# Small products of the heads, placed one by one between the products of a weight stream

## The chip, the cores and the metric

The kernel runs on one core of one Trainium2 chip. The metric is device time in microseconds. The kernel before takes 2738.81 us (median of 3 runs, 2738.59 to 2742.34).

TensorE (PE) multiplies and writes to PSUM; VectorE (DVE), ScalarE (ACT) and GpSimd (POOL) work on SBUF and PSUM; SyncE (SP) issues the transfers. Each engine takes its instructions in order and waits on semaphores of the others.

## The reference

Two layers of a decoder are computed for a prompt of 256 tokens and eight samples of 8 tokens, 320 columns in all, with shared weights. All is float32.

```python
def mixer(h, s_gla, buf, pos0, w_in, ...):
    proj = h @ w_in                       # q, k, v, g, gates, pooling input
    ...
    o, s_new = gla(q, k, v, gk, s_gla)    # 4 heads, state 128 x 256 a head
    o = rmsnorm(o, gla_norm).reshape(B, T, GLA_WIDTH) * jax.nn.silu(g)
    p, buf_new = pool_mixer(u, buf, pos0, w_pool, pool_scale)
    out = jnp.concatenate([o, p.astype(o.dtype)], axis=-1) @ w_out
    return out, s_new, buf_new

def gla step:                             # by chunk of tokens
    o_intra = einsum('bhij,bhjv->bhiv', scores, vi)
    o_inter = einsum('bhid,bhdv->bhiv', qi * exp(b), S)
    S_new = exp(b_last)[..., None] * S + einsum('bhjd,bhjv->bhdv', k_dec, vi)

def layer:
    x = x + mixer(rmsnorm(x, norm_mix[l]), ...)
    h = rmsnorm(x, norm_ffn[l])
    x = x + (silu(h @ w_gate[l]) * (h @ w_up[l])) @ w_down[l]
```

The width of the model is 2048, a head's v is 256 wide and its k 128, the FFN is 5632 wide. Outputs are the tokens, the heads' states of the prompt and of each sample, and the pooling buffers.

## The kernel before

Activations are held transposed: a tile is 128 features by 320 tokens. A *unit* is a block of weights, four row tiles by 256 columns (512 KB), which serves two output tiles. To keep float32 accuracy at the rate of a shorter format, a weight block is split into a high and a low part (`hl`): ScalarE makes the high part (L109), VectorE the low part (L110). Each product is then three matmuls, high by high, high by low, low by high (`mm3`, L145 to L147), of 320 columns each: a unit of four row tiles has 2 x 4 x 3 = 24 of them. These are the *stream products* (`acc<-xh,hl` and the like in the rows).

`run` goes through the list of units. For unit i it issues the loads of weights up to five units ahead, the split of unit i + 2, the evictions that are due, the 24 matmuls, and then `step`, which lets every generator in `gens` go on to its next `yield`. So the work that isn't part of the stream is issued between units, in the order in which the generators stand in the list. The order is fixed when the program is built; there is no scheduler.

The heads' work is such a generator (`head_gen`), one for each of four heads in each layer. It issues on TensorE:

- ten transposes of v (`ps_vt`, `ps_vs`, `ps_vq`, L651 to L657);
- three units later the output `ps_o`, in two halves of 128 rows: a product of 64-row weights (L700), eight products of 8 columns, one for a sample's state each (L702), and two for the prompt (L704, 256 columns, and L705, 128 columns); behind them two state products of 512 columns (`ps_sn`, L683). A plain float32 product shows as two passes in the rows;
- two units later the sum of squares for the head's norm (`ps_or`, L716), two products of the prompt's state (`ps_sp`, L719) and two more state products.

The other engines follow in between: ScalarE copies v and o out of PSUM (L667 to L670, L710, L711) and the prompt's state (L724), VectorE updates the samples' states (`S`, L691), `rsqrt` makes the norm (L133 to L138), GpSimd multiplies (L730). With the last step `st["head"]` is counted up, and the next head may load its states and transpose.

`gate_gen` multiplies a head's o with silu(g) (GpSimd, L748) and, a unit later, splits the product into `oh` and `ol` (L120, L125). The units of `w_out` come after those of `w_in`: first four units that read the pooling half (`ph`, `pl`), then four that read the gated heads (`oh`, `ol`), and so on.

The PSUM tiles of the small work come from a pool of four (`smt`), those of the stream from another of four.

Of the kernel before, what the change touches and what calls it, by code (L numbers as in the profile page):

```python
# [35 lines left out]
# columns of `vecs`, one 128-row column per feature tile  # L36
# [5 lines left out]
# pairs of 128-column tiles of w_in, in the order in which they are multiplied  # L42
# [10 lines left out]


class Unit:
    """A block of weights: nk row tiles by 256 columns, used by two output tiles."""
# [7 lines left out]
class Decoder:  # L64
    def __init__(self, tc, ctx, a):
        self.tc, self.nc, self.a = tc, tc.nc, a
        nc = self.nc
        pool = lambda name, bufs, **k: ctx.enter_context(tc.tile_pool(name=name, bufs=bufs, **k))
        self.const = const = pool("const", 1)
        self.act = pool("act", 1)  # L70
        self.ffb = pool("ffb", 2)
        self.wp = pool("wp", 1)
        self.nrm = pool("nrm", 1)
        self.keep = pool("keep", 1)
        self.acc = pool("acc", 4, space=PSUM)
        self.sm = pool("sm", 4, space=PSUM)

        self.vecs = const.tile([P, V_N], F32, name="vecs")
        nc.sync.dma_start(out=self.vecs, in_=a["vecs"])
        self.xT = self.act.tile([P, KT, T], F32, name="xT")  # L80
        self.xh = self.act.tile([P, KT, T], F32R, name="xh")
        self.xl = self.act.tile([P, KT, T], F32R, name="xl")
        self.ident = const.tile([P, P], F32, name="ident")
        self.ones = const.tile([P, P], F32, name="ones")
        self.masks = const.tile([P, 5 * 128 + 256], U8, name="masks")
        small = const.tile([P, 8], F32, name="small")
        self.sel4, self.warm, self.eps = small[:, 0:4], small[:, 4:5], small[:, 5:6]
        self.wcnt = const.tile([P, 4, 16], F32, name="wcnt")
        self.sc = self.keep.tile([P, H, 384], F32, name="sc")
        self.scs = self.keep.tile([64, H, 64], F32, name="scs")  # L90
        nc.gpsimd.memset(self.eps, EPS)
        self.last_sq, self.mf = [], None
        self.units = []
        self.gens = []
        self.later = []

# [8 lines left out]
    def split(self, hi, lo, src, scale=None):  # L105
        """hi + lo = src * scale, each of them with the 12 bits that the array multiplies."""
        nc = self.nc
        if scale is None:
            nc.scalar.copy(hi, src)  # L109
            nc.vector.tensor_tensor(lo, src, hi.bitcast(F32), ALU.subtract)  # L110
        else:
            nc.scalar.activation(hi, src, AF.Copy, scale=scale)  # L112
            nc.vector.scalar_tensor_tensor(lo, src, scale, hi.bitcast(F32), ALU.mult, ALU.subtract)  # L113

    def split2(self, his, los, srcs, scales=(None, None)):
        """Two splits, so that neither engine waits for the other's half."""
# [12 lines left out]
    def rsqrt(self, out, src, scale):  # L129
        """out = 1 / sqrt(src * scale + EPS): exp(-log / 2), then a Newton step."""  # L130
# [18 lines left out]
    def pair_units(self, srcs, order, rhs, evac, nk=4):  # L149
        """Units that make one pair of output tiles: srcs[i] holds row tiles 4 i .. 4 i + 3."""  # L150
        box = {}
        units = []
        for n, i in enumerate(order):
            def mm(hl, n=n, i=i):
                if n == 0:
                    box["ps"] = [self.acc.tile([P, 512], F32, tag="acc", name="acc") for _ in range(2)]
                for j in range(2):
                    for k in range(nk):
                        xh, xl = rhs(i * nk + k)
                        self.mm3(box["ps"][j][:, :T], hl, k, j, xh, xl,  # L160
                                 n == 0 and k == 0, n == len(order) - 1 and k == nk - 1)
            ev = (lambda: evac([t[:, :T] for t in box["ps"]])) if n == len(order) - 1 else None
# [45 lines left out]

    def step(self):
# [7 lines left out]
    def add_square(self, m, x):  # L217
        """Adds x * x into the running sum over feature tiles."""
# [9 lines left out]
    def make_r(self):  # L228
        """After the last square: r = rsqrt(mean + eps) on every partition."""
# [7 lines left out]
    def new_x(self, ms, l, base):  # L237
        """Two tiles of x are final: the operands with the next norm's weight, and the squares."""
# [13 lines left out]
    def mixer_units(self, l):  # L252
# [22 lines left out]
        # w_out: the pooling half of the rows first  # L275
# [51 lines left out]
    def gk_gen(self, l):  # L327
        """log of the gates: P = 16 * gk = log_sigmoid(z), z = h w_gk w_gk_up + b."""
# [6 lines left out]
        # [hi | lo] of a row tile side by side: one pass multiplies both  # L335
# [31 lines left out]
    def level_gen(self):  # L367
        """Scores k_j . q_i exp(b_i - b_j) for j <= i, transposed. Tokens are halved again and
        again: at level s, a pair with i in the second and j in the first half of a group of 2 s
        takes exp(sum from the half's start to i) on q and exp(sum from j to the half's end) on k,  # L370
        so that no exponent is above zero."""
# [31 lines left out]
        for li, s in enumerate((1, 2, 4, 8, 16, 32, 64, 128)):  # L403
# [30 lines left out]
            if s == 4:  # L434
                # whole sequences of the sample group
# [45 lines left out]
        # k decayed to the end of the prompt  # L481
# [30 lines left out]
    def kd_sample(self):  # L512
        """k decayed to the end of its sequence, as 32 rows a sequence: hi, lo, hi, lo."""
# [22 lines left out]
    def stack(self, x, out, his, los):  # L536
        """x [P, n, 8, 8] into out [P, n, 8, 4, 8] as rows hi (at his) and lo (at los)."""
# [10 lines left out]
    # -- pooling  # L548
# [16 lines left out]
    def pool_gen(self, l, i, EP, ES):  # L565
# [4 lines left out]
        # sums over trailing windows, doubling; only what the last one needs  # L570
# [13 lines left out]
        # the sequence's start: fewer positions than the window  # L584
        nc.gpsimd.tensor_tensor(cp[:, :, BUF : BUF + 16], cp[:, :, BUF : BUF + 16],
                                self.wcnt[:, i : i + 1, :].to_broadcast([P, 2, 16]), ALU.mult)
        # the buffers that go on: the last 15 rows
# [35 lines left out]
    # -- values and gates, one head at a time  # L623
# [7 lines left out]
    def head_gen(self, h, vT):  # L631
# [15 lines left out]
        p1, p2, p3 = self.smt("ps_vt"), self.smt("ps_vs"), self.smt("ps_vq")  # L647
        for c in range(2):
            for t in range(2):
                o = 256 * t + 128 * c  # L650
                nc.tensor.transpose(p1[:, o : o + 128], vT[:, c, 128 * t : 128 * t + 128], self.ident)  # L651
        for c in range(2):
            nc.tensor.transpose(p2[:64, 128 * c : 128 * c + 128], vT[:, c, NP:], self.ident)
        for c in range(2):
            for t in range(2):
                o = 256 * t + 128 * c
                nc.tensor.transpose(p3[:, o : o + 128],  # L657
                                    vq[:, c, 4 * t : 4 * t + 4].rearrange("p b a t -> p (b a t)"), self.ident)
        st["turned"] += 1
        yield  # L660
# [4 lines left out]
        # rows of one sequence at a time, zero elsewhere  # L665
# [11 lines left out]
        yield  # L677

        def state_mm(qd):
            pss = []  # L680
            for half in range(2):
                pz = self.smt("ps_sn")
                nc.tensor.matmul(pz, st["kqt"][:, qd, 128 * h : 128 * h + 128],  # L683
                                 vqt[:, 2 * half : 2 * half + 2, qd, :], start=True, stop=True)
# [11 lines left out]
        pos = []  # L696
        for c in range(2):
            po = self.smt("ps_o")
            vc = slice(128 * c, 128 * c + 128)
            nc.tensor.matmul(po[:, NP:T], vs[:, vc], self.scs[:, h, :], start=True, stop=False)  # L700
            for b in range(NB):
                nc.tensor.matmul(po[:, NP + 8 * b : NP + 8 * b + 8], S[b // 4][:, b % 4, vc],  # L702
                                 st["q8"][:, h, 8 * b : 8 * b + 8], start=False, stop=(b == NB - 1))
            nc.tensor.matmul(po[:, :NP], vt[:, 0, vc], self.sc[:, h, 0:256], start=True, stop=False)  # L704
            nc.tensor.matmul(po[:, 128:NP], vt[:, 1, vc], self.sc[:, h, 256:384], start=False, stop=True)  # L705
            pos.append(po)
        pss = state_mm(0)
        yield
        for c in range(2):
            nc.scalar.activation(o[:, c, :], pos[c][:, :T], AF.Copy, scale=self.vec(l, V_GN, c))  # L710
            nc.scalar.activation(sq[:, c, :], pos[c][:, :T], AF.Square)  # L711
        nc.gpsimd.tensor_tensor(sq[:, 0, :], sq[:, 0, :], sq[:, 1, :], ALU.add)
        state_out(0, pss)
        yield
        pr = self.smt("ps_or")
        nc.tensor.matmul(pr[:, :T], self.ones, sq[:, 0, :], start=True, stop=True)  # L716
        pS = self.smt("ps_sp")
        for t in range(2):
            nc.tensor.matmul(pS[:, :DV], st["kdt"][:, t, 128 * h : 128 * h + 128], vt[:, t, :],  # L719
                             start=(t == 0), stop=(t == 1))  # L720
        pss = state_mm(1)
        yield
        sp = late.tile([P, 2, T], F32, tag="osq", name="sp")[:, 0, :DV]
# [21 lines left out]
    def gate_gen(self, ts, h):  # L745
        st = self.st
        for j, t in enumerate(ts):
# [110 lines left out]
    def build(self):  # L858
# [4 lines left out]
        # x and the first weights arrive in turn  # L863
# [8 lines left out]
        # the array's clock rises once it has been busy for a while  # L872
# [75 lines left out]
    def finish(self, evacs):  # L948
        """The last tiles of x, and the last norm."""
# [25 lines left out]
def _pairs(w, cols):  # L975
    """[L, K, N] -> [L, N/256, K/512, 128, 4 * 256]: blocks in the order of use."""
# [7 lines left out]
def _cols(v):  # L984
    """[n * 128] -> [128, n]"""
# [74 lines left out]
```

## Time and profile before

| what | value |
|---|---|
| median of the timed runs | 2738.81 us |
| profiled execution: span (the page gives no other time of it) | 2735.4 us |
| TensorE busy | 2701.1 us, 99% |
| VectorE, ScalarE, GpSimd busy | 1351.9, 1067.3, 308.4 us |
| mean granted TensorE clock | 0.985 |
| HBM | 148 GB/s over the span |

A busy TensorE here only means that instructions follow each other without a gap; at the lower of its two clock levels it is as busy. The granted clock has to be read beside it, by stretch. In the list of instructions the given duration of a matmul overlaps with the next one, so that steps from start to start, or the chain of waits, tell what one takes.

### The profile page before, as it was taken

To read this page: it belongs to the slowest core of one execution; us is meant where nothing else is said; L and a number is where in the kernel's file an instruction comes from. 1 tells how busy PE (TensorE), PEld (TensorE's weight loads), DVE (VectorE), ACT (ScalarE), POOL (GpSimd) and SP (SyncE) were. 2 spreads that over 40 slices of the span, in tenths; PEclk is the share of its full clock that TensorE was granted. 3 is DMA by queue.
4 is the path that set the end of the run, shared out by engine and by line. 5 is a ranking of instruction groups with operands and counts; after the bars stand their busy time and mean duration, and the time that the engine had idled before them with its cause. 6 is when DMAs were issued, how large, how long until landed. Compare 5 with 4: busy or idle time off the path is not lost.

```text
span 2735.4 us, 44895 instructions
## 1 busy us (share of the span) xinstructions
PE 2701.1 (99%) x19046; PEld 2680.6 (98%) x19046; DVE 1351.9 (49%) x1654; ACT 1067.3 (39%) x1344; POOL 308.4 (11%) x347
## 2 busy tenths in 40 slices
PE   8999999999999999999999999999999999999997
PEld 8999999999999999999999999999999999999997
DVE  6764455444444444444658544544444444444444
ACT  5444544333333333333444554443333333333334
POOL 3521111000000000000106211100000000000002
PEclk9999999999999999999999999999999999999998
DMA  5345544444444444444443544544444444444443
GB/s 189 117 155 166 161 151 147 153 148 150 151 148 153 147 152 148 149 152 147 148 140 108 184 162 142 154 147 148 153 147 152 149 151 150 149 153 147 152 149 108
DMA packets 115929, 408.67 MB, mean 149 GB/s; under 512 B 13264, under 2 KB 16848, under 8 KB 115728
## 3 DMA queue, kind: packets, MB, share of 16 engines
q1 hardware_dynamic: 115728, 405.80, 47.5%
q8 instruction: 149, 2.44, 0.4%
q14 instruction: 52, 0.43, 0.0%
HBM read 392.59 MB, written 13.16 MB: 148 GB/s over the span
## 4 chain that ended last, share of the span: by engine, by line
PE 95%; DVE 2%; issue 1%; POOL 1%; ACT 0%; DMA 0%; DVEq 0%; SPq 0%; ACTq 0%; POOLq 0%
PE acc L145 30%; PE acc L147 30%; PE acc L146 30%; PE ps_o L702 1%; DVE hl L110 1%; PE ps_o L704 0%; DVE xl L113 0%; PE ps_sn L683 0%; POOL PX L430 0%; POOL AS L579 0%; POOL AP L578 0%; PE ps_sp L719 0%; PE ps_o L700 0%; PE ps_o L705 0%; DVE xT L963 0%
## 5 line engine op out<-in xcount | busy, mean ns | idle before, releaser
L110 DVE TENSOR_TENSOR hl<-raw,hl 128x1024 fp32r<-128x1024 f32 (+1 forms) x729 | 921.7, 1265 | 1258.1 <-ACT hl L109 1257.3
L109 ACT CAST hl<-raw 128x1024 fp32r<-128x1024 f32 (+1 forms) x729 | 759.9, 1043 | 1312.7 <-PE acc L147 1232.9
L145 PE MATMUL acc<-xh,hl 128*128 128x320 f32 x3840 | 1195.7, 311 | 1.0 <-ACT xh L112 0.6
L147 PE MATMUL acc<-xh,hl 128*128 128x320 f32 x3840 | 1191.2, 310 | 2.7 <-DVE hl L110 2.7
L146 PE MATMUL acc<-xl,hl 128*128 128x320 f32 x3840 | 1191.5, 310 | 2.4 <-DVE xl L113 2.4
L145 PEld LDWEIGHTS acc<-xh,hl 128*128 128x128 f32 x3840 | 726.0, 189 | 4.3 <-ACT PX L359 0.9
L146 PEld LDWEIGHTS acc<-xl,hl 128*128 128x128 f32 x3840 | 725.5, 189 | 4.1 <-DVE xl L113 2.7
L147 PEld LDWEIGHTS acc<-xh,hl 128*128 128x128 f32 x3840 | 725.1, 189 | 3.8 <-DVE hl L110 3.7
L147 PE MATMUL acc<-ah,hl 128*128 128x320 f32 x1408 | 435.1, 309 | 0.0
L145 PE MATMUL acc<-ah,hl 128*128 128x320 f32 x1408 | 435.1, 309 | 0.0
L146 PE MATMUL acc<-al,hl 128*128 128x320 f32 x1408 | 435.1, 309 | 0.0
L145 PEld LDWEIGHTS acc<-ah,hl 128*128 128x128 f32 x1408 | 264.3, 188 | 0.0
L146 PEld LDWEIGHTS acc<-al,hl 128*128 128x128 f32 x1408 | 264.3, 188 | 0.0
L147 PEld LDWEIGHTS acc<-ah,hl 128*128 128x128 f32 x1408 | 264.3, 188 | 0.0
L783 POOL TENSOR_TENSOR ft<-ft,r 128x320 f32<-128x320 f32 x88 | 75.5, 880 | 1641.2 <-ACT ft L782 1629.4
L249 DVE TENSOR_TENSOR xT<-xT,acc 128x320 f32<-128x320 f32 x224 | 98.4, 481 | 5.8 <-PE acc L147 5.8
L226 POOL TENSOR_TENSOR sqa<-sqa,sq 128x320 f32<-128x320 f32 x58 | 51.0, 880 | 309.1 <-ACT sq L225 307.0
L145 PE MATMUL acc<-ph,hl 128*128 128x320 f32 x256 | 79.1, 309 | 0.0
L146 PE MATMUL acc<-pl,hl 128*128 128x320 f32 x256 | 79.1, 309 | 0.0
L147 PE MATMUL acc<-ph,hl 128*128 128x320 f32 x256 | 79.1, 309 | 0.0
L145 PE MATMUL acc<-oh,hl 128*128 128x320 f32 x256 | 79.1, 309 | 0.0
L146 PE MATMUL acc<-ol,hl 128*128 128x320 f32 x256 | 79.1, 309 | 0.0
(197 smaller groups left out, 1604.9 us busy)
## 6 DMA issues: line engine op xcount, KB each, us to landing
raw<-in_w_gu SPq DMA_DIRECT2D x352, 512.0 KB, 3.6
raw<-in_w_down SPq DMA_DIRECT2D x176, 512.0 KB, 3.6
raw<-in_w_in SPq DMA_DIRECT2D x127, 512.0 KB, 3.8
raw<-in_w_out SPq DMA_DIRECT2D x64, 512.0 KB, 3.7
S<-in_s SPq DMA_DIRECT2D x16, 512.0 KB, 4.8
out_s_sample<-S SPq DMA_DIRECT2D x16, 512.0 KB, 2.9
raw<-in_w_pool SPq DMA_DIRECT2D x8, 256.0 KB, 2.8
xT<-in_xT SPq DMA_DIRECT2D x3, 640.0 KB, 7.2
```

Source lines behind the costliest of these rows:

```text
L109: nc.scalar.copy(hi, src)
L110: nc.vector.tensor_tensor(lo, src, hi.bitcast(F32), ALU.subtract)
L145: nc.tensor.matmul(ps, wh, xh, start=first, stop=False)
L146: nc.tensor.matmul(ps, wh, xl, start=False, stop=False)
L147: nc.tensor.matmul(ps, wl, xh, start=False, stop=last)
L226: nc.gpsimd.tensor_tensor(self.sq_acc, self.sq_acc, s, ALU.add)
L249: self.nc.vector.tensor_tensor(self.xT[:, m, :], self.xT[:, m, :], p, ALU.add)
L702: nc.tensor.matmul(po[:, NP + 8 * b : NP + 8 * b + 8], S[b // 4][:, b % 4, vc], st["q8"][:, h, 8 * b : 8 * b + 8], start=False, stop=(b == ...
L783: self.nc.gpsimd.tensor_tensor(t, t, self.r, ALU.mult)
```

## The change

`head_gen` doesn't issue its products any more. It puts them into a queue (`add_small`) with a number for each, a cost in ns. `beside`, called after every three stream products, adds 260 to a credit and takes pieces from the queue while the credit is above zero; each takes its number off. The generator then waits (`placed`) until the queue is empty. The order of the output's products within a half is turned round: the prompt's come first, then the 64-row product and the eight of 8 columns. One `yield` less stands before the output. The first two state products are queued after the output's are placed. `gate_gen` waits until its head's o is there. Comments are gone too, which moves line numbers.

```diff
+BESIDE = 260
...
+        self.small = collections.deque()
+        self.credit = 0
...
                         self.mm3(box["ps"][j][:, :T], hl, k, j, xh, xl,
                                  n == 0 and k == 0, n == len(order) - 1 and k == nk - 1)
+                        self.beside()
...
+    def add_small(self, ns, f):
+
+        self.small.append((ns, f))
+
+    def beside(self):
+        if not self.small:
+            self.credit = 0
+            return
+        self.credit = min(self.credit, 0) + BESIDE
+        while self.small and self.credit > 0:
+            ns, f = self.small.popleft()
+            self.credit -= ns
+            f()
+
+    def placed(self):
+
+        while self.small:
+            yield
...
+        turn = lambda o, x: self.add_small(110, lambda: nc.tensor.transpose(o, x, self.ident))
...
-                nc.tensor.transpose(p1[:, o : o + 128], vT[:, c, 128 * t : 128 * t + 128], self.ident)
+                turn(p1[:, o : o + 128], vT[:, c, 128 * t : 128 * t + 128])
...
+        yield
+        yield from self.placed()
         st["turned"] += 1
-        yield
...
         yield
-        yield
...
-                nc.tensor.matmul(pz, st["kqt"][:, qd, 128 * h : 128 * h + 128],
-                                 vqt[:, 2 * half : 2 * half + 2, qd, :], start=True, stop=True)
+                self.add_small(230, lambda pz=pz, half=half: nc.tensor.matmul(
+                    pz, st["kqt"][:, qd, 128 * h : 128 * h + 128],
+                    vqt[:, 2 * half : 2 * half + 2, qd, :], start=True, stop=True))
...
-        pos = []
-        for c in range(2):
+        def out_mm(c):
             po = self.smt("ps_o")
             vc = slice(128 * c, 128 * c + 128)
-            nc.tensor.matmul(po[:, NP:T], vs[:, vc], self.scs[:, h, :], start=True, stop=False)
+            self.add_small(450, lambda: nc.tensor.matmul(
+                po[:, :NP], vt[:, 0, vc], self.sc[:, h, 0:256], start=True, stop=False))
+            self.add_small(220, lambda: nc.tensor.matmul(
+                po[:, 128:NP], vt[:, 1, vc], self.sc[:, h, 256:384], start=False, stop=True))
+            self.add_small(220, lambda: nc.tensor.matmul(
+                po[:, NP:T], vs[:, vc], self.scs[:, h, :], start=True, stop=False))
             for b in range(NB):
-                nc.tensor.matmul(po[:, NP + 8 * b : NP + 8 * b + 8], S[b // 4][:, b % 4, vc],
-                                 st["q8"][:, h, 8 * b : 8 * b + 8], start=False, stop=(b == NB - 1))
-            nc.tensor.matmul(po[:, :NP], vt[:, 0, vc], self.sc[:, h, 0:256], start=True, stop=False)
-            nc.tensor.matmul(po[:, 128:NP], vt[:, 1, vc], self.sc[:, h, 256:384], start=False, stop=True)
-            pos.append(po)
+                self.add_small(224, lambda b=b: nc.tensor.matmul(
+                    po[:, NP + 8 * b : NP + 8 * b + 8], S[b // 4][:, b % 4, vc],
+                    st["q8"][:, h, 8 * b : 8 * b + 8], start=False, stop=(b == NB - 1)))
+            return po
...
+        pos = [out_mm(0), out_mm(1)]
+        yield
+        yield from self.placed()
         pss = state_mm(0)
-        yield
         for c in range(2):
-            nc.scalar.activation(o[:, c, :], pos[c][:, :T], AF.Copy, scale=self.vec(l, V_GN, c))
-            nc.scalar.activation(sq[:, c, :], pos[c][:, :T], AF.Square)
+            out(c, pos[c])
         nc.gpsimd.tensor_tensor(sq[:, 0, :], sq[:, 0, :], sq[:, 1, :], ALU.add)
+        yield
+        yield from self.placed()
         state_out(0, pss)
-        yield
         pr = self.smt("ps_or")
-        nc.tensor.matmul(pr[:, :T], self.ones, sq[:, 0, :], start=True, stop=True)
+        self.add_small(540, lambda: nc.tensor.matmul(pr[:, :T], self.ones, sq[:, 0, :], start=True, stop=True))
...
+            self.add_small(430, lambda t=t: nc.tensor.matmul(
+                pS[:, :DV], st["kdt"][:, t, 128 * h : 128 * h + 128], vt[:, t, :], start=(t == 0), stop=(t == 1)))
         pss = state_mm(1)
         yield
+        yield from self.placed()
...
     def gate_gen(self, ts, h):
         st = self.st
+        while h not in st["o"]:
+            yield
```

On TensorE, the output of the first head of the first layer (`acc` is the stream, `ps_o` the head's output, `ps_sn` a state product). Before:

```order
L147 MATMUL acc<-xh,hl 128x320
L700 MATMUL ps_o<-scs,vs 128x64
L702 MATMUL ps_o<-q_155,S 128x8 x8
L704 MATMUL ps_o<-sc,vt 128x256
L705 MATMUL ps_o<-sc,vt 128x128
L700 MATMUL ps_o<-scs,vs 128x64
L702 MATMUL ps_o<-q_155,S 128x8 x8
L704 MATMUL ps_o<-sc,vt 128x256
L705 MATMUL ps_o<-sc,vt 128x128
L683 MATMUL ps_sn<-vqt,kqt 128x512 x2
L145 MATMUL acc<-xh,hl 128x320
```

On TensorE in the new kernel, a stretch from the middle of the same head's output, where the first half ends and the second begins:

```order
L732 MATMUL ps_o<-q_155,S 128x8
L150 MATMUL acc<-xh,hl 128x320
L151 MATMUL acc<-xl,hl 128x320
L152 MATMUL acc<-xh,hl 128x320
L725 MATMUL ps_o<-sc,vt 128x256
L150 MATMUL acc<-xh,hl 128x320
L151 MATMUL acc<-xl,hl 128x320
L152 MATMUL acc<-xh,hl 128x320
L150 MATMUL acc<-xh,hl 128x320
L151 MATMUL acc<-xl,hl 128x320
L152 MATMUL acc<-xh,hl 128x320
L727 MATMUL ps_o<-sc,vt 128x128
```

The burst's 22 output products are spread over 57 stream products, mostly one behind each three; the two state products follow 15 stream products later.

On ScalarE, the end of the last head of the first layer (`sp` is the prompt's state, `rs_` the norm, `oh` the gated head, `hl` the split of a weight block). Before:

```order
L724 COPY sp<-ps_sp 128x256
L133 ACT_TABLE_LOAD
L133 ACTIVATE rs_t<-ps_or,small 128x320
L134 ACT_TABLE_LOAD
L134 ACTIVATE rs_y<-rs_t 128x320
L109 CAST hl<-raw 128x1024 x2
L742 ACT_TABLE_LOAD
L742 ACTIVATE gt<-gt 128x320 x2
L109 CAST hl<-raw 128x1024
L120 CAST oh<-gt 128x320 x2
L109 CAST hl<-raw 128x1024 x5
```

And on ScalarE in the new kernel, the same place:

```order
L761 COPY sp<-ps_sp 128x256
L138 ACT_TABLE_LOAD
L138 ACTIVATE rs_t<-ps_or,small 128x320
L139 ACT_TABLE_LOAD
L139 ACTIVATE rs_y<-rs_t 128x320
L114 CAST hl<-raw 128x1024
L125 CAST oh<-gt 128x320 x2
L114 CAST hl<-raw 128x1024 x4
```

The cast of the gated head stands one weight split behind the norm instead of three, the silu has moved ahead, and four splits instead of five are left before the first eviction of `w_out`: the head ends nearer to the units that read it.

## Rows read from the trace of the kernel before

**Rows 1.** The page: busy time of the engines, and TensorE's clock in 40 slices

```profile
PE 2701.1 (99%) x19046; PEld 2680.6 (98%) x19046; DVE 1351.9 (49%) x1654; ACT 1067.3 (39%) x1344; POOL 308.4 (11%) x347
...
PEclk9999999999999999999999999999999999999998
```

**Rows 2.** TensorE's longest wait in total: us, times, longest us

```profile
PE acc L145 <- DVE ES L560: 6.4, 2, 3.4
```

**Rows 3.** Stretches: us, TensorE busy (instructions), clock, DMA share, GB/s

```profile
190.00:210.00 20.00, 20.00 (x119) 0.83 0.33 106
224.00:244.00 20.00, 20.00 (x127) 0.91 0.38 116
```

**Rows 4.** Chain of waits, third burst of the first layer: start us, us, what

```profile
260.81 1.88 PE ps_o L702 x16
262.69 0.53 PE ps_o L704 x2
263.22 0.22 PE ps_o L705 x2
...
263.80 3.48 PE ps_o L702 x16
267.29 1.05 PE ps_o L704 x2
268.34 0.43 PE ps_o L705 x2
268.76 0.85 PE ps_sn L683 x2
269.62 0.27 PE acc L145
```

**Rows 5.** Chain of waits, last group of the fourth head of the first layer

```profile
314.44 0.54 PE ps_or L716 x2
314.97 0.86 PE ps_sp L719 x4
315.84 0.45 PE ps_sn L683 x2
316.29 0.15 PE acc L145
```

**Rows 6.** Chain of waits, second burst, its second half and the stream behind

```profile
231.67 2.19 PE ps_o L702 x16
...
236.20 0.27 PE acc L145
```

**Rows 7.** TensorE in order of time, lone product at 35.57: start us, us, instruction

```profile
35.42 0.31 PE L147 MATMUL acc<-xh,hl 128*128 128x320 f32 x1
...
36.26 0.30 PE L146 MATMUL acc<-xl,hl 128*128 128x320 f32 x1
```

**Rows 8.** TensorE in order of time, the first burst's entry

```profile
192.68 0.31 PE L145 MATMUL acc<-xh,hl 128*128 128x320 f32 x1
...
194.29 0.31 PE L147 MATMUL acc<-xh,hl 128*128 128x320 f32 x1
194.53 0.43 PE L700 MATMUL ps_o<-scs,vs 64*128 64x64 f32 x2
```

**Rows 9.** ScalarE, VectorE, GpSimd in order of time, last head's end

```profile
315.93 0.37 ACT L724 COPY sp<-ps_sp 128x256 f32<-128x256 f32 x1 [0.37 <-PE ps_sp L719]
...
321.58 2.64 POOL L730 TENSOR_TENSOR o<-o,ro 128x320 f32<-128x320 f32 x2 [12.28 <-DVE ro L138]
326.72 1.72 POOL L748 TENSOR_TENSOR gt<-gt,o 128x320 f32<-128x320 f32 x2 [2.50 <-ACT gt L742]
...
328.47 0.46 ACT L120 CAST oh<-gt 128x320 fp32r<-128x320 f32 x1 [0.18 <-POOL gt L748]
330.45 1.05 ACT L109 CAST hl<-raw 128x1024 fp32r<-128x1024 f32 x1 [1.52 <-PE acc L147]
...
331.54 1.23 DVE L110 TENSOR_TENSOR hl<-raw,hl 128x1024 fp32r<-128x1024 f32 x1 [1.21 <-ACT hl L109]
```

More of the change, by code (lines that the diff above doesn't have):

```diff
@@ L1 @@
+import collections
 from contextlib import ExitStack
@@ L650, in head_gen @@
                 o = 256 * t + 128 * c
-                nc.tensor.transpose(p1[:, o : o + 128], vT[:, c, 128 * t : 128 * t + 128], self.ident)
+                turn(p1[:, o : o + 128], vT[:, c, 128 * t : 128 * t + 128])
         for c in range(2):
-            nc.tensor.transpose(p2[:64, 128 * c : 128 * c + 128], vT[:, c, NP:], self.ident)
+            turn(p2[:64, 128 * c : 128 * c + 128], vT[:, c, NP:])
         for c in range(2):
@@ L656, in head_gen @@
                 o = 256 * t + 128 * c
-                nc.tensor.transpose(p3[:, o : o + 128],
-                                    vq[:, c, 4 * t : 4 * t + 4].rearrange("p b a t -> p (b a t)"), self.ident)
+                turn(p3[:, o : o + 128], vq[:, c, 4 * t : 4 * t + 4].rearrange("p b a t -> p (b a t)"))
+        yield
+        yield from self.placed()
         st["turned"] += 1
-        yield
         while not st.get("levels"):
@@ L707, in head_gen, with out @@
+        def out(c, po):
+            nc.scalar.activation(o[:, c, :], po[:, :T], AF.Copy, scale=self.vec(l, V_GN, c))
+            nc.scalar.activation(sq[:, c, :], po[:, :T], AF.Square)
+        pos = [out_mm(0), out_mm(1)]
+        yield
+        yield from self.placed()
         pss = state_mm(0)
+        for c in range(2):
+            out(c, pos[c])
+        nc.gpsimd.tensor_tensor(sq[:, 0, :], sq[:, 0, :], sq[:, 1, :], ALU.add)
         yield
-        for c in range(2):
-            nc.scalar.activation(o[:, c, :], pos[c][:, :T], AF.Copy, scale=self.vec(l, V_GN, c))
-            nc.scalar.activation(sq[:, c, :], pos[c][:, :T], AF.Square)
@@ L712, in head_gen @@
-        nc.gpsimd.tensor_tensor(sq[:, 0, :], sq[:, 0, :], sq[:, 1, :], ALU.add)
+        yield from self.placed()
         state_out(0, pss)
-        yield
         pr = self.smt("ps_or")
-        nc.tensor.matmul(pr[:, :T], self.ones, sq[:, 0, :], start=True, stop=True)
+        self.add_small(540, lambda: nc.tensor.matmul(pr[:, :T], self.ones, sq[:, 0, :], start=True, stop=True))
         pS = self.smt("ps_sp")
         for t in range(2):
-            nc.tensor.matmul(pS[:, :DV], st["kdt"][:, t, 128 * h : 128 * h + 128], vt[:, t, :],
-                             start=(t == 0), stop=(t == 1))
+            self.add_small(430, lambda t=t: nc.tensor.matmul(
+                pS[:, :DV], st["kdt"][:, t, 128 * h : 128 * h + 128], vt[:, t, :], start=(t == 0), stop=(t == 1)))
```

## The prediction

> **What bounds the kernel now.** I read the page first. TensorE is busy for 2701 of 2735.4 us, and its clock row shows a 9 in almost every slice [rows 1]. The reader should see that a slice is 68 us, so a short fall of the clock can't be seen there. The list of TensorE's waits comes next: its longest total is 6.4 us [rows 2], so there is no stall for the change to take away, and a gain has to come from TensorE's own work, either from its amount or from its speed. So the granted clock around the heads' products decides. There are eight such places, four heads in each of two layers. In 20 us around the first of them the mean granted clock is 0.83, around the second 0.91 [rows 3]. With the two levels of 2.4 and 1.2 GHz that is (1 - 0.83) x 20 x 2 = 6.8 us and 3.6 us at the low level. The same view gives 0.83 around six of the eight and 0.91 around two.
>
> The chain of waits then shows what that costs, since it gives each group the time that it really takes. In the third burst [rows 4] the first half runs at the high clock: sixteen passes of 8 columns (two passes for each of eight products) in 1.88 us, the 256-column product in 0.53, the 128-column one in 0.22. The second half, the same work, takes 3.48, 1.05 and 0.43; after it the state products take 0.85 and the first four stream products 0.27 each, before the stream is back at 0.15 [rows 5]. In front of the fall stand the burst's own products, most of them 8 columns wide; TensorE has no gap there. The other two groups of a head (ten transposes; the norm's sum with two state products) are short: in the last group three kinds take 0.54, 0.86 and 0.45 and the stream goes on at 0.15 [rows 5].
>
> **The change part by part.** The number of instructions of TensorE stays: per head 10 transposes, 22 products for the output, 4 for the sample state, 1 for the norm, 2 for the prompt state, 312 in all. What changes is where they stand: in 24 groups before, in 232 groups now, most of them a single product behind three stream products.
>
> *The clock.* What the low clock costs in the third burst: 3.48 - 1.88 = 1.60; 1.05 - 0.53 = 0.52; 0.43 - 0.22 = 0.21; the two state products 0.85 - 0.45 = 0.40 [rows 4, 5]; four stream products at 0.27 in place of 0.15 make 0.48. Sum 3.21 us. In the second burst the fall comes late, in the second half's passes (2.19 in place of 1.88: 0.31), then 0.52 + 0.21 + 0.40 as before, and one stream product at 0.27 makes 0.12 [rows 6]: 1.56 us. Six bursts of the first kind and two of the second: 6 x 3.21 + 2 x 1.56 = 22.4 us. In the new order a product of 8 columns, which costs 1.88/8 = 0.235 us, has 0.44 us of full stream products ahead of it and behind it, so some two thirds of the time is stream. I take it that the clock stays up, since it stayed up with the stream around every short group [rows 5].
>
> *The small work itself.* Does a product that stands alone cost what it costs in a burst? The nearest row is the norm's sum of a layer, one 32-bit product of two passes between stream products [rows 7]: from the product ahead of it (start 35.42) to the second behind it (36.26) are 0.84 us; two stream steps of 0.146 (eleven of them in 1.61 us, from 192.68 to 194.29 [rows 8]) are 0.29, which leaves 0.55, and the same two passes inside a group take 0.54 [rows 5]. So entering and leaving costs nothing that can be seen, and spreading 312 products adds nothing. From the other side: the product with 64-row weights starts 0.24 us behind the stream product before it instead of 0.15 [rows 8]. That 0.09 is there in both orders for those sixteen products. If it came at each of the 208 new entries it would cost 18.7 us, and with as much on the way back 37 us. I take 0, by the row of the lone product, whose weights have 128 rows like most of what is moved. Below nothing: the 256-column pair behind the short passes takes 0.53 [rows 4], while four passes of 256 columns in the last group take 0.86, 0.43 a pair [rows 5]; in the new order that product stands behind a stream product, and if the 0.10 goes it is 1.6 us over sixteen pairs. I leave it out of the sum and keep it for the range.
>
> *Steps that move.* A head now needs seven units of stream from its transposes to its last step instead of six, because the output's products fill two and a half units. Between heads this is covered by the stream. A new wait could arise where the next head's transposes reuse a PSUM buffer: they follow the last state product by six stream products (0.9 us) instead of 24. They wait for ScalarE's copy of the prompt state and, the last of them, for VectorE's update of the sample state. With 24 products of cover no such wait is among TensorE's [rows 2], so the 18 lost can cost 18 x 0.146 = 2.6 us at most at each of six places, 16 us in all; both begin while the group is still being placed, and I count nothing. SyncE's loads of the next head's state and of weights change places by two rows, and the weights are loaded about three units, over 10 us, ahead: nothing.
>
> *The last head's tail.* Here the cover shrinks. Before, 168 stream products lay between the last state product and the second w_out unit that reads the gated heads; now 75 do, 75 x 0.146 = 11.0 us. The chain that has to fit, in durations of before [rows 9]: from ScalarE's copy at 315.93 to GpSimd's first step with the norm at 321.58, 5.65 us; its two pairs of steps 2.64 and 1.72; ScalarE's cast 0.46; then, queued behind it on ScalarE, that unit's weight split, 1.05, and VectorE's half, 1.23: 12.7 us. The copy starts before the last state product does, since it waits for a product further ahead: nine stream products and a state product lie between, 9 x 0.146 + 0.22 = 1.5 us, less the 0.1 us from that product's end to the copy [rows 5, 9]. So 12.7 - 1.4 = 11.3 against 11.0 plus the state product's own 0.22 and two stream products, 0.29: even. If it is late, TensorE waits at that unit's third product and all behind it is queued. I take 0.25 us for each of two layers, 0.5 in all, with ends of 0 and 3.
>
> Sum: -22.4 + 0.5 = -21.9 us on a span of 2735.4, so 2713.5 us of span. The median of the timed runs is 3.4 us above the profiled span; what lies around a span has no part in the change, so the time is 2738.8 - 21.9 = **2717 us**, 0.8% less.
>
> The Trainium skill (TensorE: Matmul & The Clock Gate, "Why this matters for your kernels") ties the fall of the clock to gaps in which TensorE is idle between bursts, and warns of such gaps. This trace does not agree: the clock falls while the engine is issuing, with 16 passes in 1.88 us just before [rows 4]. By the page's wording there would be no gap to close here and the sum would have no clock term; I go by the rows.
>
> **The rivals.**
> 1. *Entries cost something.* A part of the 0.09 us of the 64-row product comes at every change between stream and small product. At 0.05 us, 208 x 0.05 = 10.4 us come back: 2727. The gain is used up at 21.9/208 = 0.105 us an entry. For it: [rows 8]. Against it: [rows 7]. Chance 8%.
> 2. *New waits.* The tail is late by its end of 3 us in all, and the transposes by a fifth of their bound, 3 us: 6 us more, 2723. For it: the tail's cover is even with its chain. Chance 7%.
> 3. *Slower: the mixture itself is too thin and the clock is low all through it.* Each head's output is spread over 57 stream products. At the low clock they cost 0.12 more each, 6.8 us, and the two halves of the output some 2.5 us more each (by the third burst 1.60 + 0.52 + 0.21 = 2.3 and the 64-row product): 12 us a head, 94 us in all, against 22.4 saved: 2811. It decides when two or more of the eight heads fall so. Against it: the clock stays up after the shorter groups, and two thirds of the new stretch are stream products. Chance 3%.
> 4. *No change.* The falls have another cause than what the bursts are made of; they stay where the heads' output stands and only move with it: 2739, within a few us. For it: the trace shows where they lie, not why. Against it: in the two bursts shown the clock falls only once the short passes have run for 3 us, and the shorter groups cause none. Chance 4%. The page's rule named above would lead here, since it speaks of idle gaps alone.
>
> **How the numbers follow.** The forecast has 78%. Its own spread comes from where in a burst the clock falls, which differs between executions as between these eight bursts: all of the short kind give 8 x 1.56 = 12.5 us, all of the long kind 8 x 3.21 = 25.7. So 2738.8 - 25.7 - 1.6 = 2711 at the low end. At the high end 2738.8 - 12.5 = 2726, and rivals 1 and 2 lie at 2727 and 2723; the range is 2711 to 2727. A change under 0.2%, 5.5 us, is about what a measurement of this kernel can't tell from none. Faster: the forecast, rival 2 and most of rival 1, 0.92; same: rival 4, 0.04; slower: rival 3 and the rest of rival 1, 0.04.
>
> **What would show it.** Right: the mean granted clock is 1.00 in every 20 us of both head stretches, and the two stretches are 11 us shorter each; stream steps of 0.146 us between small products; a lone 8-column product lengthens the chain by 0.22 to 0.24 us. The tail shows as a TensorE wait for VectorE's or ScalarE's weight split in w_out's sixth unit, under 1 us. Wrong: a clock below 1 in those stretches (rivals 3, 4), a step onto or off an 8-column product longer than its two passes (rival 1), or new TensorE waits of several us in sum (rival 2).

## The result, and the profile after

The changed kernel takes 2714.5 us (median of four runs, 2713.6 to 2714.8) beside 2738.7 us for the kernel before: ratio 0.991, interval 0.990 to 0.992. Forecast were 2717 us and a range of 2711 to 2727. The profiled span fell from 2735.4 to 2713.1 us, 22.3 us less; forecast were 21.9.

The page of the changed kernel (busy time of the engines; TensorE's clock in 40 slices) answers to [rows 1].

```profile
PE 2675.9 (99%) x19046; PEld 2655.7 (98%) x19046; DVE 1349.9 (50%) x1654; ACT 1066.4 (39%) x1344; POOL 311.6 (11%) x347
...
PEclk9999999999999999999999999999999999999999
```

The number of TensorE's instructions is the same, its busy time 25 us less, the other engines' within 4 us: the same work runs faster. The view by stretches shows where. First the two stretches of [rows 3] in the changed kernel, then both head stretches whole (stretch, length and TensorE's busy time, clock, DMA share, GB/s):

```profile
190.00:210.00 20.00, 20.00 (x141) 1.00 0.36 106
224.00:244.00 20.00, 20.00 (x140) 1.00 0.45 155
...
182.00:322.00 140.00, 140.00 (x956) 1.00 0.51 168
1533.00:1673.00 140.00, 140.00 (x954) 1.00 0.50 163
```

The same two long stretches of the kernel before:

```profile
182.00:322.00 140.00, 140.00 (x880) 0.91 0.49 159
1533.00:1673.00 140.00, 140.00 (x880) 0.91 0.48 158
```

With two levels, 0.09 x 140 x 2 is 25 us at the low level in each, at which half the work gets done, so by this estimate some 12.6 us were lost in each: about what was won. The starts of products in time order give it closer. From the first head's first transpose to the first stream product that reads the gated heads (acc<-oh) it took 154.46 and 154.41 us in the two layers before, and 142.79 and 142.78 after. In the new order the first transposes start behind three more stream products, 0.44 us later, so 11.23 and 11.19 us are gone: 22.4 us. The other stages kept their length within 0.2 us: 105.6 us from there to the norm, 877.02 us from the first layer's FFN to the second layer's gates, 844.80 us from the second FFN to the last norm, in both kernels.

The chain of waits in the third head's output shows the new order (start us, us, what). L725, L727, L729 and L732 are the products that were L704, L705, L700 and L702.

```profile
259.90 0.43 PE ps_o L725 x2
260.33 0.15 PE acc L150
...
260.77 0.22 PE ps_o L727 x2
...
261.43 0.36 PE ps_o L729 x2
261.80 0.35 PE acc L150
...
262.43 0.12 PE ps_o L732 x2
262.55 0.25 PE acc L150
...
263.09 0.12 PE ps_o L732 x2
```

Against [rows 4] there is no doubled number left. An 8-column product takes 0.12 us, and the stream product behind it 0.25 instead of 0.147: 0.22 us in all. The 64-row product takes 0.36 and delays the stream product behind it by 0.20: 0.56 us. The 256-column pair takes 0.43 and the 128-column one 0.22.

TensorE's waits (us in total, times, longest us) answer to [rows 2]; no head or tail work is among them.

```profile
PE acc L150 <- DVE ES L585: 6.5, 2, 3.3
PE acc L152 <- DVE hl L115: 4.5, 4, 1.6
```

The first lies in the stage of the levels and the pooling, ahead of the heads. Of the second, 3.1 us fall into the first 30 us of the program and the rest into that same stage of both layers. The end of the last head, in time order on ScalarE, GpSimd and VectorE, answers to [rows 9]:

```profile
317.29 0.37 ACT L761 COPY sp<-ps_sp 128x256 f32<-128x256 f32 x1 [2.12 <-PE ps_sp L755]
...
322.94 2.63 POOL L767 TENSOR_TENSOR o<-o,ro 128x320 f32<-128x320 f32 x2 [12.90 <-DVE ro L143]
325.54 1.71 POOL L787 TENSOR_TENSOR gt<-gt,o 128x320 f32<-128x320 f32 x2
...
327.65 1.99 ACT L114 CAST hl<-raw 128x1024 fp32r<-128x1024 f32 x2
...
328.73 3.59 DVE L115 TENSOR_TENSOR hl<-raw,hl 128x1024 fp32r<-128x1024 f32 x3 [0.46 <-ACT hl L114]
```

The first of VectorE's three splits there ends at about 328.73 + 3.59/3 = 329.93. TensorE's product that needs it is the third of its unit, L152 at 330.11, and it starts on its beat:

```profile
329.96 0.31 PE L151 MATMUL acc<-ol,hl 128*128 128x320 f32 x1
330.11 0.31 PE L152 MATMUL acc<-oh,hl 128*128 128x320 f32 x1
```

The steps are 0.147 us ahead of it, so it did not wait, with some 0.18 us to spare.

### The profile page after: what moved, and what is told of

It is laid out like the page before. It is cut to its first block, busy times and chain, and to the rows that moved or that the text cites. A ratio compares the mean times of both kernels' runs of the same rounds, so it can differ in the third digit from the quotient of the medians.

```text
span 2713.1 us, 44884 instructions
## 1 busy us (share of the span) xinstructions
PE 2675.9 (99%) x19046; PEld 2655.7 (98%) x19046; DVE 1349.9 (50%) x1654; ACT 1066.4 (39%) x1344; POOL 311.6 (11%) x347
## 4 chain that ended last, share of the span: by engine, by line
PE 94%; DVE 2%; issue 1%; POOL 1%; ACT 1%; DMA 0%; DVEq 0%; SPq 0%; ACTq 0%; POOLq 0%
PE acc L150 31%; PE acc L152 30%; PE acc L151 30%; DVE hl L115 1%; PE ps_o L732 1%; POOL PX L455 0%; POOL AS L604 0%; POOL AP L603 0%; PE ps_sn L708 0%; PE ps_sp L755 0%; PE ps_o L725 0%; ACT hl L114 0%; DVE xl L118 0%; PE ps_o L729 0%; DVE xT L1002 0%
## 5 line engine op out<-in xcount | busy, mean ns | idle before, releaser
L152 PE MATMUL acc<-xh,hl 128*128 128x320 f32 x3840 | 1187.9, 309 | 4.5 <-DVE hl L115 4.5
L152 PEld LDWEIGHTS acc<-xh,hl 128*128 128x128 f32 x3840 | 721.2, 188 | 6.2 <-DVE hl L115 6.1
L152 PE MATMUL acc<-ah,hl 128*128 128x320 f32 x1408 | 435.1, 309 | 0.0
L152 PEld LDWEIGHTS acc<-ah,hl 128*128 128x128 f32 x1408 | 264.3, 188 | 0.0
L822 POOL TENSOR_TENSOR ft<-ft,r 128x320 f32<-128x320 f32 x88 | 75.5, 881 | 1641.2 <-ACT ft L821 1641.2
L150 PE MATMUL acc<-oh,hl 128*128 128x320 f32 x256 | 79.1, 309 | 0.0
L152 PE MATMUL acc<-oh,hl 128*128 128x320 f32 x256 | 79.1, 309 | 0.0
L152 PE MATMUL acc<-ph,hl 128*128 128x320 f32 x256 | 79.1, 309 | 0.0
```

The source lines that it names most:

```text
L150: nc.tensor.matmul(ps, wh, xh, start=first, stop=False)
L152: nc.tensor.matmul(ps, wl, xh, start=False, stop=last)
L822: self.nc.gpsimd.tensor_tensor(t, t, self.r, ALU.mult)
```

## The experiments

The theory was: what the change earns is TensorE's clock in the heads' output bursts, and nothing else. The rivals: the new order of the products earns it, the placing by itself, or some other edit. Later the question became what in a burst lets the clock fall.

**1. The queue in bursts.** All edits of the change stay, but a burst leaves the queue at once.

```diff
-BESIDE = 260
+BESIDE = 100000
```

> The changed kernel with every edit kept (queue, order of the products, yields, gate's wait), except that the credit per three stream products is without limit, so that all pieces that stand in the queue come in one burst at the next place. Theory, the clock: TensorE's granted clock falls again in the heads' output bursts, some 0.91 in each of the two head stretches instead of 1.00, and the time goes back by about 22 us, to 2736 (2727 to 2739). Rival, the other edits or the new order earn the gain: the time stays at 2714.5 within 2 us and the stretches stay at 1.00.

Measured: 2737.8 us, ratio to the kernel before 0.9996 (0.9986 to 1.0005). The gain is gone. The chain of waits in the second head, with the prompt's products first:

```profile
223.38 0.43 PE ps_o L725 x2
...
224.39 1.88 PE ps_o L732 x16
226.27 0.53 PE ps_o L725 x2
226.81 0.22 PE ps_o L727 x2
227.03 0.36 PE ps_o L729 x2
227.39 2.26 PE ps_o L732 x16
229.65 0.47 PE acc L150
230.11 0.27 PE acc L151
```

The first half is fast; the clock falls within the second half's short passes (2.26 instead of 1.88), and the stream behind goes at 0.27. Over the two head stretches the clock is 0.90 and 0.91. Generators, waits and the order inside a half earn nothing without the spreading.

**2. The new order alone, in the kernel before.** In each half the two prompt products go ahead of the sample products.

```diff
+            nc.tensor.matmul(po[:, :NP], vt[:, 0, vc], self.sc[:, h, 0:256], start=True, stop=False)
+            nc.tensor.matmul(po[:, 128:NP], vt[:, 1, vc], self.sc[:, h, 256:384], start=False, stop=True)
             nc.tensor.matmul(po[:, NP:T], vs[:, vc], self.scs[:, h, :], start=True, stop=False)
...
-            nc.tensor.matmul(po[:, :NP], vt[:, 0, vc], self.sc[:, h, 0:256], start=True, stop=False)
-            nc.tensor.matmul(po[:, 128:NP], vt[:, 1, vc], self.sc[:, h, 256:384], start=False, stop=True)
```

> The kernel before with one edit: in each half of a head's output the prompt's two products (256 and 128 columns) come first and the 64-row and the eight 8-column products behind them, as in the changed kernel; all still in one burst. Theory, the clock: 16 products of 8 columns are still in one burst, the clock still falls in the heads; 2738 (2734 to 2741), at most 1.6 us less from the pair of 256 columns. Rival, the order inside a half earns the gain: 2714 to 2718.

Measured: 2737.3 us, ratio 0.9994 (0.9984 to 1.0003); clock 0.91 and 0.93 in the head stretches. The order is not it.

**3 and 4. Both kernels without the 8-column products.**

```diff
-            nc.tensor.matmul(po[:, NP:T], vs[:, vc], self.scs[:, h, :], start=True, stop=False)
-            for b in range(NB):
-                nc.tensor.matmul(po[:, NP + 8 * b : NP + 8 * b + 8], S[b // 4][:, b % 4, vc],
-                                 st["q8"][:, h, 8 * b : 8 * b + 8], start=False, stop=(b == NB - 1))
+            nc.tensor.matmul(po[:, NP:T], vs[:, vc], self.scs[:, h, :], start=True, stop=True)
```

The kernel before:

> The kernel before without the 128 products of 8 columns (the samples' part that comes from the old state is left out of the output); bursts and order stay. Warm, the 128 products are worth 128 x 0.224 = 28.7 us. Theory, the 8-column products in a row are what lets the clock fall: no falls in the heads, so 2738.8 - 28.7 - 22.4 = 2688 (2685 to 2691), and the clock is 1.00 in both head stretches. Rival, the burst as such lets it fall, whatever stands in it: falls stay, 2705 to 2711.

The changed kernel:

> The changed kernel without the 128 products of 8 columns (the samples' part that comes from the old state is left out of the output). Theory, the queue earns only the clock: without these products queue and bursts are the same, 2714.5 - 28.7 = 2685.8 (2684 to 2688), beside 2685.3 of the kernel before without them. Rival, placing the pieces between stream products is worth something by itself, or costs something: more than 2 us off 2685.3.

Measured: 2685.3 us (2684.5 to 2688.4) and 2687.4 us (2686.4 to 2688.2). Without the 8-column products the bursts keep the clock at 1.00 in both head stretches, here those of the kernel before:

```profile
182.00:322.00 140.00, 140.00 (x926) 1.00 0.57 186
1533.00:1673.00 140.00, 140.00 (x933) 1.00 0.56 181
```

The kernel before is 54 us faster than beside it with them (2739.4): 29 is what the products themselves are worth, by experiment 5, and 25 the clock. The change then earns nothing. The 2.0 us between the two medians are just past the bound that the rival was given, but they don't come from the heads: from first transposes to acc<-oh it is 128.93 and 128.94 us before, 128.49 and 128.47 with the queue, plus the 0.44 by which its first transposes stand later: equal within 0.03. The profiled executions are 3.4 us apart. Of that 1.6 us lie in the program's start (46.28 and 47.90 us to the first product of the gates) and 2.0 in the second layer's level stage, ahead of the heads, which took 135.46 and 137.86 us (0.44 of it are the later transposes). This stage varies in all kernels (135.5 to 140.1 in the eleven experiments).

**5. The bursts of before, with wider products.** Place, number and weights of the 128 products stay; each multiplies 64 columns instead of 8.

```diff
-                nc.tensor.matmul(po[:, NP + 8 * b : NP + 8 * b + 8], S[b // 4][:, b % 4, vc],
-                                 st["q8"][:, h, 8 * b : 8 * b + 8], start=False, stop=(b == NB - 1))
+                nc.tensor.matmul(po[:, NP:T], S[b // 4][:, b % 4, vc],
+                                 st["q8"][:, h, :], start=False, stop=(b == NB - 1))
```

> The kernel before with the 128 products of 8 columns made 64 columns wide (each sequence's state times all 64 sample columns, all into the same 64 columns, so the samples' outputs hold other sums); number, place and weight loads of the products stay. The 64-row product of 64 columns takes 0.22 us beside 0.224 us of an 8-column one, so warm time should stay the same. Theory A, the burst lets the clock fall because its products have few columns: no falls, 2738.8 - 22.4 = 2716 (2713 to 2722), clock 1.00 in the head stretches. Theory B, it falls because the stream stops for some 7 us: falls stay, 2738 (2735 to 2742), clock 0.91.

Measured: 2714.4 us (2714.2 to 2715.1), ratio 0.991 (0.989 to 0.993): the whole gain of the change, without queue or new order. The second burst in the chain of waits:

```profile
225.97 1.93 PE ps_o L702 x16
227.90 0.49 PE ps_o L704 x2
...
228.61 0.36 PE ps_o L700 x2
228.97 1.93 PE ps_o L702 x16
230.90 0.49 PE ps_o L704 x2
231.38 0.22 PE ps_o L705 x2
231.60 0.47 PE ps_sn L683 x2
```

Eight times the columns cost 0.05 us in 1.9, and nothing doubles in the second half. (The expectation gave the 64-row product 0.22 us; in the chain it takes 0.36, here and in the kernel before. What was to stay the same, the time of a wide product, is 1.93/8 = 0.24.) The stream stands still for 6.5 us here too, so it is not the pause of the stream that lets the clock fall. By the starts of the stream products on either side (from the one ahead to the second behind, less their own steps), each of the eight bursts delays the stream by 6.46 or 6.47 us; before it was 7.7 to 9.3. All small work of the heads together delays it by 75.3 us here and by 75.4 us in the changed kernel: spread or in bursts at a high clock, it costs the same.

**6. The change with twice the credit.**

```diff
-BESIDE = 260
+BESIDE = 520
```

> The changed kernel with the credit per three stream products doubled (260 to 520), so that two or three pieces enter between the same three stream products instead of one or two. Theory, thin work in sum lets the clock fall: the mixture holds more of it, so the clock falls in some bursts or in none; 2713 to 2736, and whatever the time is above 2714 it is low clock in the head stretches, not stalls. Rival, only an unbroken burst lets it fall: 2714 (2712.5 to 2715.5) and 1.00 in both stretches.

Measured: 2714.9 us (2713.8 to 2715.1), clock 1.00 in both stretches, 75.5 us of delay. Groups of two or three pieces keep the clock. Both readings allowed this time, so this run doesn't choose between them; it shows that the setting isn't delicate.

**7. 128 rows in the changed kernel.** The 64-row product adds 0.56 us where others add 0.22. Its weights and the scores get 64 rows of zeros.

```diff
-        self.scs = self.keep.tile([64, H, 64], F32, name="scs")
+        self.scs = self.keep.tile([P, H, 64], F32, name="scs")
...
-        vs = late.tile([64, DV], F32, tag="vs", name="vs")
+        vs = late.tile([P, DV], F32, tag="vs", name="vs")
+        nc.gpsimd.memset(vs[64:], 0.0)
...
-        nc.scalar.copy(vs, p2[:64, :DV])
+        nc.scalar.copy(vs[:64], p2[:64, :DV])
```

> The changed kernel with one edit: the weights of the 64-row product (vs, and the scores scs that it multiplies) get 128 rows, the lower 64 of them zero, so that every product of the program has 128 rows. In the trace after, the 64-row product alone between stream products adds 0.56 us, the 8-column and 128-column ones with 128 rows 0.22 us. Theory, the step between 64 and 128 rows is what costs 0.34 us more: 16 x 0.34 = 5.4 us less, 2709 (2708 to 2710.5), each such piece then adds 0.22 us. Rival, the product costs this wherever and however it stands: 2714.5 within 1.5.

Measured: 2709.8 us (2709.1 to 2710.9), ratio 0.989 (0.988 to 0.991); all its runs lie under all those of the changed kernel. The chain of waits in the third head:

```profile
260.17 0.17 PE ps_o L730 x2
260.34 0.20 PE acc L150
260.54 0.14 PE acc L151
```

0.17 and 0.20 stand in place of 0.36 and 0.35. From first transposes to acc<-oh each layer is 2.67 us shorter (142.78 to 140.11), 5.3 in all as expected. This version beats both kernels.

**8 and 9. Wide products with the sums kept, in the bursts of before.** Zero-padded queries make the 8-column products 32 columns wide. Number 8 does this alone, number 9 also gives the weights 128 rows as above.

```diff
+        qz = self.nrm.tile([P, T], F32, tag="sq", name="qz", bufs=2).rearrange("p (g c) -> p g c", g=2)
+        nc.gpsimd.memset(qz, 0.0)
...
-                nc.tensor.matmul(po[:, NP + 8 * b : NP + 8 * b + 8], S[b // 4][:, b % 4, vc],
-                                 st["q8"][:, h, 8 * b : 8 * b + 8], start=False, stop=(b == NB - 1))
+                nc.tensor.matmul(po[:, NP + 32 * (b // 4) : NP + 32 * (b // 4) + 32], S[b // 4][:, b % 4, vc],
+                                 qz[:, b // 4, 32 * (b % 4) : 32 * (b % 4) + 32], start=False, stop=(b == NB - 1))
```

Number 8:

> The kernel before with the 128 products of 8 columns made 32 columns wide with zeros in the 24 columns of the other sequences; the sums stay what they were, bursts and order too. Theory, thin products in a row let the clock fall: 64 columns held it at 1.00 (2714.4); with 32 columns, 2714 to 2717 if that is wide enough, anything up to 2738 with falls in some bursts if not. Rival, a burst must stand between stream products to be fast: 2738.

Number 9:

> The kernel before (bursts, no queue) with two edits: the 128 products of 8 columns become 32 columns wide, with zeros in the 24 columns of the other sequences (one tile of zero-padded queries per head, made on GpSimd), and the 64-row weights get 128 rows, half of them zero. If four times the columns keep the clock up in a burst and the rows are worth 5.4 us as expected of the changed kernel: 2714.4 - 5.4 = 2709 (2708 to 2712). If 32 columns are too few and the clock falls: 2722 to 2734. If the rows are worth nothing in a burst: 2714.5.

Measured: 2739.5 us for number 8 (one of ten runs at 2725.8, nine from 2737.9 to 2743.6), and 2710.5 us (2708.9 to 2711.3) for number 9. I had expected some gain of number 8; nine of the ten runs show none, and in the profiled one all eight bursts fall. The rival, that a burst must stand between stream products to be fast, goes with this time too, but number 5 rules it out: it is a burst, and fast. The second burst of number 8, second half:

```profile
232.09 0.36 PE ps_o L705 x2
232.46 3.09 PE ps_o L707 x16
235.55 1.01 PE ps_o L709 x2
236.56 0.43 PE ps_o L710 x2
```

The same half in number 9:

```profile
227.33 0.17 PE ps_o L706 x2
227.50 1.76 PE ps_o L708 x16
229.26 0.51 PE ps_o L710 x2
229.77 0.22 PE ps_o L711 x2
```

With 128 rows a half takes 2.66 us instead of 3.00 and the clock stays. So the 64-row products count in the fall as well, beyond their own 0.34 us.

**10 and 11. Are the 64-row products the trigger?** Number 10 is the kernel before with the edit of number 7 alone, number 11 the kernel before without the 64-row products:

```diff
-            nc.tensor.matmul(po[:, NP:T], vs[:, vc], self.scs[:, h, :], start=True, stop=False)
...
-                                 st["q8"][:, h, 8 * b : 8 * b + 8], start=False, stop=(b == NB - 1))
+                                 st["q8"][:, h, 8 * b : 8 * b + 8], start=True, stop=True)
```

Number 10:

> The kernel before with one edit: the weights of the 64-row product get 128 rows, the lower 64 zero; the products of 8 columns and the bursts stay. With 32 columns and these 128 rows the clock stayed at 1.00 (2710.5), with 32 columns and 64 rows it fell (2739.5). Theory A, the two 64-row products of a burst are what lets the clock fall: no falls, 2738.8 - 5.4 - 22.4 = 2711 (2709 to 2714). Theory B, it falls for thin work in sum, and rows and columns each bring some of it: with 8 columns the falls stay, 2733 (2728 to 2736).

Number 11:

> The kernel before without the 16 products of 64 rows (the samples' part from within their own eight tokens is left out of the output); the 128 products of 8 columns and the bursts stay. Warm, the 16 products are worth 16 x 0.56 = 9.0 us. Theory A, the 64-row products let the clock fall: 2738.8 - 9.0 - 22.4 = 2707 (2705 to 2711). Theory B, thin work in sum: the falls stay in most bursts, 2730 (2720 to 2733).

Measured: 2721.0 us (2718.8 to 2727.6) and 2718.0 us (2715.5 to 2720.1). Each lies between its two expectations: about half of the time that the falls cost is won. Number 10 in the first layer, by stretches that hold the burst of the first, second, third and fourth head (stretch, length and TensorE's busy time, clock, DMA share, GB/s):

```profile
185.00:225.00 40.00, 40.00 (x281) 1.00 0.52 173
225.00:255.00 30.00, 30.00 (x212) 1.00 0.56 181
255.00:290.00 35.00, 35.00 (x221) 0.90 0.49 164
290.00:325.00 35.00, 35.00 (x232) 0.95 0.44 143
```

The first two bursts are undisturbed and the last two are not, though their instructions are the same (the second and third begin up to 0.4 us ahead of their stretch). Of the eight in both layers four delay the stream by the undisturbed 5.79 us and four by 6.7 to 7.9; in number 11 it is 5.34 us in two and 6.2 to 7.7 in six. Neither the 8-column nor the 64-row products are the sole trigger: the clock still falls in four of eight bursts with 128 rows and in six of eight without these products, and with the 64 rows it doesn't fall where the other products are 64 wide (number 5) or left out (number 3). Why bursts of the same instructions differ within one execution is open.

## Why the prediction was right

*No stall to take away, so the clock decides.* Held. Experiments 1 and 5 show it from both sides: the change without the spreading earns nothing, and a high clock without the change earns everything.

*The clock term, -22.4 us.* Held: 22.4 us in the two stages, none anywhere else. That six bursts counted with 3.21 and two with 1.56 us came so close is partly luck. Against the undisturbed 6.46 us of number 5 the eight bursts of the kernel before, in its profiled execution, cost 1.3 to 2.8 us too much, 16.7 in sum; the rest lies in the stream products behind them.

*The small work at nothing.* Held: 75.4 us of delay spread, 75.3 in bursts at the high clock. The 0.09 us at the 64-row product is there, and more behind it, but in either order: 128 rows saved 5.3 us in the new order (number 7 against the change, by the stages) and 0.34 us in each of the sixteen halves of the bursts (2.66 in number 9 against 3.00 in number 5). The 0.10 us kept below nothing for the 256-column pair (0.53 to 0.43) is seen, but belongs to the products around it and not to the sum: the half as a whole takes 3.00 us in number 5 with its pair at 0.49.

*New waits at the transposes: nothing.* Held: no such row among TensorE's waits.

*The last head's tail, 0.5 us.* Judged even, and it is, with 0.18 us to spare, so the 0.5 was not paid: that is about what lies between the forecast span, 2713.5 us, and the measured one.

*From span to time.* The step that was furthest off, by 2 us: "the median of the timed runs is 3.4 us above the profiled span; what lies around a span has no part in the change". In every run listed with both numbers the time is about 1.8 us above its own span. The rest of the 3.4 was that the profiled execution was one of the faster ones. The kernel before spread from 2735.6 to 2741.2 us over the 39 runs beside the experiments, the changed kernel from 2713.6 to 2714.8 over four. Of the 39, those with a higher mean clock were faster on average (2737.2 us at 0.987, 2738.9 at 0.986, 2740.0 at 0.985), so at least part of the spread seems to come from where in the bursts the clock fell, and it went with the falls. So the median gained 24.2 us where the span gained 22.3.

*The rivals.* Entry costs: nothing by the two sums. New waits: none, by the list of TensorE's waits. Slower through a thin mixture: the clock is 1.00 all through it, and still with double the credit. No change: the gain came, and experiments 1 and 5 tie the falls to what the bursts are made of. TensorE has no gap in the bursts, with or without a fall: number 5 and the kernel before have the same group at the same place, and one keeps the clock while the other loses it. So the rule of the Trainium skill (TensorE: Matmul & The Clock Gate, "Why this matters for your kernels"), that idle gaps let the clock fall, does not explain these falls. One argument against this rival was misread: that the clock falls "only once the short passes have run for 3 us". In the third burst 3.48 beside 1.88 in [rows 4] is nearly a doubling of the whole second half, so only about 2 us of short passes had run when the clock fell.

*Beyond the prediction.* I took the short passes for the cause and the stream around them for the cure. The first is half the story: 64-row weights and few columns both count. How the two add up is open. In the profiled executions 32 columns with 64 rows fell as often as 8 columns with 64 rows (all eight bursts), while 8 columns with 128 rows fell in four; these don't order by columns alone or by rows alone.

## What to carry to other kernels

Look at the granted clock around groups of thin products even where TensorE shows no gap, and price a fall from the same products at both levels, the stream behind them included. Two cures gave nearly the same time here: spreading the group through a full stream, and making its products wider and taller with zeros (2709.8 and 2710.5 us, both with 128-row weights). The zeros cost little: sixteen passes of 64 columns took 1.93 us where sixteen of 8 columns took 1.88. Where the time varies from one execution to the next, as here with the falls, set the profiled span against the run that it belongs to, not against the median of others.

## What the runs showed of the hardware

A product with 64-row weights among products of 128 rows took 0.56 us, and 0.22 us with 64 zero rows added, both alone between stream products (0.36 + 0.35 against 0.17 + 0.20 in the chain, less the stream product's own 0.147). The Trainium skill (TensorEngine Tiling (Array Packing), "Key Properties") says that a change of the array's tiling mode drains TensorE; the trace agrees as far as it goes, since the time is lost on entering and on leaving (0.36 against 0.17 and 0.35 against 0.20), though no run here shows the mode.

A 32-bit product of 8 columns took as long as one of 64: 1.88 and 1.93 us for eight of them, 2.41 and 2.42 with the 256-column pair behind.
